# Stick-breaking attention: all projections behind the weighted sums and dealt 3, 4, 6, 7; scores seven tiles ahead; one block of h read back from DRAM

## The chip, the cores and the metric

One Trainium2 chip, one core. The metric is the device time of one execution in microseconds (us). The kernel before took 1917.51 us, the median of 3 runs.

## What is computed

One layer of a decoder trunk on 2048 tokens of width 1024: h is the RMS-normed and modulated x, p = h @ w_in feeds two groups of 8 heads of 64, an RWKV-7 recurrence and a stick-breaking attention, each gated; both go through w_out. The change sits in the attention and in the projections that run beside it.

```python
def stick_breaking_group(p, sb_g):
    q, k, v, g = jnp.split(p, 4, axis=-1)
    ...
    def block(args):
        z = jnp.einsum('bhqd,bhkd->bhqk', q_blk, k).astype(jnp.float32) * scale
        mask = k_pos[None, :] < q_pos[:, None]
        log_1m = jnp.where(mask, jax.nn.log_sigmoid(-z), 0.0)
        after = lax.cumsum(log_1m, axis=3, reverse=True) - log_1m
        attn = jnp.where(mask, jnp.exp(jax.nn.log_sigmoid(z) + after), 0.0)
        return jnp.einsum('bhqk,bhkd->bhqd', attn.astype(v.dtype), v)
    ...
    o = rmsnorm(o, sb_g.reshape(H, N)).reshape(B, S, SB_WIDTH)
    return o * jax.nn.silu(g)
```

## The kernel before

The program has three stretches. The **setup** (0 to 139 us) reads x and the modulation weights, makes h in four blocks of 512 tokens (`make_h`, L262), each as a float16 high part `hh` and low part `hl` of 1 MB that stay in SBUF for the whole program (`hth`, `htl`), and projects q, k, v of the first two blocks. The **attention** (139 to 1045 us) follows, then a second scheduling context with the **RWKV** group and the output projection (1045 to 1918 us).

The attention runs in 16 steps n = 4j + b: j is a pair of heads, b a block of 512 queries. Step n has 8(b+1) items (8, 16, 24, 32). An item is one score tile and one weighted-sum tile, on every engine:

- `scores` (L481): TensorE makes z with two matmuls (L492, L493) into one of 3 PSUM buffers; ScalarE takes two sigmoids, u (L496) and s (L497); GpSimd copies a carry (L507); VectorE runs the cumulative product over u (L505 on the diagonal, L508 elsewhere); GpSimd multiplies it onto s (L509). s has NS = 8 buffers, u has NU = 5.
- `turn` (L514): TensorE transposes up to four 128x128 pieces of s into one of 2 PSUM buffers `tr` (L521); ScalarE copies them out as the high part ah (L525), VectorE makes the low part al (L526).
- `weigh` (L529): TensorE adds ah and al times v into av (L539, L540). It comes LAG = 3 items after its turn.

`attend` (L573) emits per item the scores of the item LEAD = 5 places later, a turn and a weigh. It reaches into the next step except from a step with b = 0, whose successor starts with five score tiles of its own. When a step's second head is done, VectorE writes L550 and TensorE transposes the result (L558, `otp`).

Beside it `fill` (L633) emits the projections: k, q, v of a later step, the gates "g" (attention) and "r" (RWKV) of four blocks each, and, in the last step, four shifted projections z (`pss`). A projection (`inproj`, L351) is 8 pieces of 3 matmuls 128x512. Per head pair 20 of them are dealt to the four steps as 4, 4, 6, 6; the step n = 2 has 3. `_merge` interleaves both lists by planned work, and the scheduler, which runs a timeline model of its own, then sets each engine's order. `pace` (L349) is a scheduling bound: no piece is placed ahead of the weighted sum emitted last before it. It is set from step 12 on (L541) and only for `inproj`, not for `inproj_tok`, which makes v:

```python
        ins = PE.matmul(av[:, r], vs, al[:, r], start=False, stop=last, skip_group_check=True)
        if n >= 12:
            pace[0] = ins.ins
```

All loads and stores named here are issued by SyncE (SP), in order, on one queue.

Of the kernel before, what the change touches and what calls it, by code (L numbers as in the profile page):

```python
# [63 lines left out]
class _Slots:  # L64
# [6 lines left out]
    def tile(self, shape, dtype, name, tag=None, bufs=None):  # L71
        tag = tag or name
        n = self.bufs if bufs is None else bufs
        ring = self.rings.setdefault(tag, [[], 0])
        size = math.prod(shape[1:]) * (2 if dtype in (F16, BF16) else 4)
        if len(ring[0]) < n:
            ring[0].append(self.used[0])
            self.used[0] += -(-size // 32) * 32
            assert self.used[0] <= 4 * self.words
        o = ring[0][ring[1] % n]  # L80
        ring[1] += 1
        key = (o, str(dtype), tuple(shape))
        if key not in self.made:
            self.made[key] = self.nc.alloc_sbuf_tensor_at(f"kept_{name}{o}", shape, dtype, offset=self.base + o)
        t = self.made[key]
        return t[tuple(slice(None) for _ in shape)]


def trunk(nc, a, out):
# [93 lines left out]
    hth, htl = [], []  # L183
    xblk = {}

# [76 lines left out]
    def make_h(b):  # L262
# [14 lines left out]
        hh = hp.tile([P, KB, TB], F16, tag="hth", name="hh")  # L277
        hl = hp.tile([P, KB, TB], F16, tag="htl", name="hl")
# [9 lines left out]
        hth.append(hh)  # L288
        htl.append(hl)
# [61 lines left out]
    def inproj(w, b, name):  # L351
        wh, wl = w[0], w[1]
        ps = mm_ps(name)
        for k in range(KB):
            with tc.issue_after(pace[0]) if pace[0] is not None else nullcontext():
                PE.matmul(ps, wh[:, k], hth[b][:, k], start=k == 0, stop=False)  # L356
            PE.matmul(ps, wh[:, k], htl[b][:, k], start=False, stop=False)  # L357
            PE.matmul(ps, wl[:, k], hth[b][:, k], start=False, stop=k == KB - 1)  # L358
            yield 0.65
        return ps  # L360

    def inproj_tok(w, b, name):
        wh, wl = w[0], w[1]
        ps = mm_ps(name)
        for i in range(4):
            t = slice(i * P, (i + 1) * P)
            for k in range(KB):
                PE.matmul(ps[:, t], hth[b][:, k, t], wh[:, k], start=k == 0, stop=False)
                PE.matmul(ps[:, t], hth[b][:, k, t], wl[:, k], start=False, stop=False)
                PE.matmul(ps[:, t], htl[b][:, k, t], wh[:, k], start=False, stop=k == KB - 1)  # L370
                if k % 4 == 3:
                    yield 0.65
        return ps
# [93 lines left out]
    NS, NU, LEAD, LAG = 8, 5, 5, 3  # L467
# [13 lines left out]
    def scores(n, i, sb):  # L481
# [13 lines left out]
        s = sb.tile([P, TB], F32, tag="s", bufs=NS, name="s")  # L495
# [33 lines left out]
    def weigh(sb, n, i, ah, al, r):  # L529
# [11 lines left out]
        if n >= 12:  # L541
            pace[0] = ins.ins
# [30 lines left out]
    def attend(n, sb):  # L573
# [59 lines left out]
    def fill(n, sb):  # L633
# [3 lines left out]
        if n < 2:  # L637
            m = n + 2
        else:
            m = n + 1 if 2 < n < NST - 1 else None  # L640
        new = b == 3 and not end
        if b == 0 and j > 0:
            yield from w_split("g", j)
# [3 lines left out]
        if b == 3:  # L647
            yield from w_split("z" if end else "k", 0 if end else j + 1)
            w_load("rk" if end else "q", 0 if end else j + 1)
        gates = [("g", 0)], [("g", 1)], [("g", 2), ("g", 3), ("r", 0)], [("r", 1), ("r", 2), ("r", 3)]  # L650
        gates = [proj_g(kind, j, gb, sb) for kind, gb in gates[b]]
        if m is not None:
            yield from proj_k(m)
            if new:
                yield from gates.pop(0)
                yield from w_split("q", j + 1)
                w_load("v", j + 1)
            yield from proj_q(m)
            if new:
                yield from gates.pop(0)  # L660
                yield from w_split("v", j + 1)
                w_load("g", j + 1)
            yield from proj_v(m)
        if j > 0:
            yield from combine(j - 1, b, sb)
        if n == NST - 1:
            for i in range(4):
                yield from proj_z(i, sb)
                if gates:
                    yield from gates.pop(0)  # L670
                if i < 3:
                    yield from w_split(("rk", "rr", "rv")[i], 0)
                if i < 2:
                    w_load(("rr", "rv")[i], 0)
        for g in gates:
            yield from g
        if b == 1:
            w_load("r", j)

    def fill_work(n):  # L680
        b = n % NB
        if n == NST - 1:
            return 5.2 * 7 + 1.5
        return 5.2 * ((4, 4, 6, 6)[b] - 3 * (n == 2)) + 0.9 * (n > 3) + (0.2, 0, 0.2, 0.6)[b]
# [509 lines left out]

    _merge((stage_pw(0), 22), (combines(), 6))
# [4 lines left out]
    def load_wout(k2):  # L1200
        wh = hp.tile([P, 2, D], F32R, tag="hth", name="woh")
        wl = hp.tile([P, 2, D], F32R, tag="htl", name="wol")
# [119 lines left out]
```

## Time and profile before

| | |
|---|---|
| median of 3 runs | 1917.51 us (1916.39 to 1922.70) |
| the profiled execution | 1919.86 us, of which 1918.1 us is the span of instructions |
| attention, 139.0 to 1045.1 us | 906.1 us |
| busy, whole span | PE 89%, DVE 72%, ACT 45%, POOL 40% |
| mean granted TensorE clock | 0.971 of 2.4 GHz |

A stretch's bound is read by putting beside its length what each engine needs for its work there. A busy TensorE is not one at its peak: matmuls overlap in the records, and an isolated one is longer than one in a row. So TensorE's work is counted from its instructions and the distance of the starts of neighbours in a dense run.

### The profile page before, as it was taken

To read this page: it belongs to the slowest core of one execution; us is meant where nothing else is said; L and a number is where in the kernel's file an instruction comes from. 1 tells how busy PE (TensorE), PEld (TensorE's weight loads), DVE (VectorE), ACT (ScalarE), POOL (GpSimd) and SP (SyncE) were. 2 spreads that over 40 slices of the span, in tenths; PEclk is the share of its full clock that TensorE was granted. 3 is DMA by queue.
4 is the path that set the end of the run, shared out by engine and by line. 5 is a ranking of instruction groups with operands and counts; after the bars stand their busy time and mean duration, and the time that the engine had idled before them with its cause. 6 is when DMAs were issued, how large, how long until landed. Compare 5 with 4: busy or idle time off the path is not lost. (4 is left out here: it accounts for less than half of the span.)

```text
span 1918.1 us, 38809 instructions
## 1 busy us (share of the span) xinstructions
PE 1699.1 (89%) x14816; PEld 1164.2 (61%) x14816; DVE 1380.4 (72%) x2871; ACT 859.7 (45%) x1706; POOL 774.4 (40%) x1114
## 2 busy tenths in 40 slices
PE   1879978999899998999997888898899998989998
PEld 1546655666565665667654455665565655667886
DVE  8967697678785778768766557878777777765543
ACT  0556576456564666546644333333332333422221
POOL 3615465356553556445444123233233322223322
PEclk9989999999999999999989989999999999999999
DMA  8341201222122221132111523322332333335442
GB/s 296 112 144 45 70 25 45 64 75 64 42 56 75 61 67 41 51 79 69 54 45 39 154 49 86 69 62 77 77 80 77 86 78 104 80 92 169 149 138 88
DMA packets 210408, 159.93 MB, mean 83 GB/s; under 512 B 113247, under 2 KB 171820, under 8 KB 210222
## 3 DMA queue, kind: packets, MB, share of 16 engines
q1 hardware_dynamic: 209220, 155.31, 28.8%
q8 instruction: 117, 1.92, 0.4%
q10 hardware_dynamic: 1002, 2.13, 0.4%
q14 instruction: 69, 0.57, 0.1%
HBM read 94.48 MB, written 44.04 MB: 72 GB/s over the span
## 5 line engine op out<-in xcount | busy, mean ns | idle before, releaser
L509 POOL TENSOR_TENSOR s<-s,u 128x512 f32<-128x512 f32 (+2 forms) x320 | 306.0, 964 | 219.6 <-ACT s L497 99.7
L526 DVE TENSOR_TENSOR al<-tr,ah 128x512 fp32r<-128x512 f32 (+1 forms) x320 | 187.3, 598 | 98.0 <-ACT ah L525 97.2
L508 DVE TENSOR_TENSOR_SCAN u<-u,dmask 128x512 f32<-128x512 f32 x192 | 239.8, 1267 | 13.7 <-ACT u L496 12.1
L525 ACT ACTIVATE ah<-tr 128x512 fp32r<-128x512 f32 (+1 forms) x320 | 171.9, 553 | 104.8 <-PE tr L521 101.5
L496 ACT ACTIVATE u<-z 128x512 f32<-128x512 f32 (+2 forms) x320 | 173.4, 556 | 73.4 <-PE z L493 48.1
L521 PE MATMUL tr<-kept_ident,s 128*128 128x128 f32 x1088 | 174.2, 280 | 32.8 <-DVE al L526 26.2
L497 ACT ACTIVATE s<-z 128x512 f32<-128x512 f32 (+2 forms) x320 | 166.2, 549 | 54.6 <-PE tr L521 54.6
L521 PEld LDWEIGHTS tr<-kept_ident,s 128*128 128x128 f32 x1088 | 130.9, 143 | 74.5 <-DVE al L526 37.5
L356 PE MATMUL pss<-kept_hh,kept_wh 128*128 128x512 f16 x416 | 160.4, 386 | 8.8 <-PEq L716 8.8
L357 PE MATMUL pss<-kept_hl,kept_wh 128*128 128x512 f16 x416 | 160.3, 385 | 0.0
L358 PE MATMUL pss<-kept_hh,kept_wl 128*128 128x512 f16 x416 | 160.3, 385 | 0.0
L358 PEld LDWEIGHTS <-kept_wl 128*128 128x128 f16 x928 | 93.3, 101 | 105.1 <-issue 14.2
L356 PEld LDWEIGHTS <-kept_wh 128*128 128x128 f16 x928 | 94.5, 102 | 101.5 <-issue 29.8
L357 PEld LDWEIGHTS <-kept_wh 128*128 128x128 f16 x928 | 93.3, 100 | 92.8 <-issue 23.1
L492 PE MATMUL z<-kt,qt 128*128 128x512 f32 (+2 forms) x320 | 132.2, 418 | 10.4 <-ACT s L497 4.4
L539 PE MATMUL av<-ah,vt 128*128 128x512 f32 (+1 forms) x320 | 136.6, 427 | 4.8 <-DVE o L550 2.3
L540 PE MATMUL av<-al,vt 128*128 128x512 f32 (+1 forms) x320 | 136.3, 427 | 0.2 <-DVE al L526 0.2
L493 PE MATMUL z<-kt,qt 128*128 128x512 f32 (+2 forms) x320 | 117.5, 371 | 0.0
L505 DVE TENSOR_TENSOR_SCAN u<-u,dmask 128x128 f32<-128x128 f32 (+3 forms) x128 | 107.2, 866 | 12.2 <-ACT u L496 6.6
L356 PE MATMUL psg<-kept_hh,kept_wh 128*128 128x512 f16 x256 | 100.4, 392 | 8.2 <-DVE klo L420 3.1
L1260 PE MATMUL po<-kept_woh,kept_yh 128*128 128x512 f32 x256 | 103.3, 404 | 0.0
L1261 PE MATMUL po<-kept_wol,kept_yh 128*128 128x512 f32 x256 | 101.9, 398 | 0.0
(292 smaller groups left out, 4167.0 us busy)
## 6 DMA issues: line engine op xcount, KB each, us to landing
kept_raw<-in_w_in SPq DMA_DIRECT2D x29, 512.0 KB, 3.9
ad<-in_ada_w SPq DMA_DIRECT2D x24, 512.0 KB, 5.4
qt<-qt SPq DMA_DIRECT2D x48, 256.0 KB, 3.4
xt<-in_x SPq DMA_DIRECT2D x16, 512.0 KB, 5.2
y<-sg SPq DMA_DIRECT2D x32, 256.0 KB, 2.0
t<-dt SPq DMA_DIRECT2D x64, 128.0 KB, 3.1
xr<-in_x SPq DMA_DIRECT2D x16, 512.0 KB, 3.6
out<-xr SPq DMA_DIRECT2D x16, 512.0 KB, 2.6
```

The source lines that it names most:

```text
L356: PE.matmul(ps, wh[:, k], hth[b][:, k], start=k == 0, stop=False)
L357: PE.matmul(ps, wh[:, k], htl[b][:, k], start=False, stop=False)
L358: PE.matmul(ps, wl[:, k], hth[b][:, k], start=False, stop=k == KB - 1)
L496: A.activation(out=u[:, 0:nk], in_=z[:, 0:nk], func=AF.Sigmoid, scale=-0.125)
L497: A.activation(out=s[:, 0:nk], in_=z[:, 0:nk], func=AF.Sigmoid, scale=0.125)
L508: V.tensor_tensor_scan(out=ur, data0=ur, data1=mr, initial=u[:, nk:nk + 1], op0=ALU.mult, op1=ALU.bypass)
L509: G.tensor_tensor(out=s[:, 0:nk], in0=s[:, 0:nk], in1=u[:, 1:nk + 1], op=ALU.mult)
L521: PE.transpose(tp[:, q * P:(q + 1) * P], att[gi, q][:, ks * P:(ks + 1) * P], ident)
L525: A.activation(out=ah[:, r], in_=tp[:, r], func=AF.Copy)
L526: V.tensor_tensor(out=al[:, r], in0=tp[:, r], in1=ah[:, r].bitcast(F32), op=ALU.subtract)
L539: PE.matmul(av[:, r], vs, ah[:, r], start=first, stop=False, skip_group_check=True)
L540: ins = PE.matmul(av[:, r], vs, al[:, r], start=False, stop=last, skip_group_check=True)
```

## The change

1. Every weighted sum sets `pace`, so all projections of the attention, v among them, are held behind the weighted sums.
2. The 20 projections of a head pair are dealt 3, 4, 6, 7; the last step gets 8 instead of 7. Their order over the blocks changes with it.
3. LEAD goes from 5 to 7, NS from 8 to 12, NU from 5 to 9. The lookahead crosses every step; it waits, in the order of emission, until the q it needs has been projected.
4. Room for it: block 3's buffers of h become eight s buffers. Setup stores each block of h to DRAM (`hd`, 2 MB a block in two DMAs) and puts block 3 where block 0 was. In each head pair block 0 is read back over block 3 in step b = 2, and block 3 over block 0 (over block 1 in the last) in step b = 3; the RWKV part begins by reading block 1 back (`h_load`, two DMAs of 1 MB each).

```diff
+    hth = [hp.tile([P, KB, TB], F16, tag="hth", name="hh") for _ in range(4)]
+    htl = [hp.tile([P, KB, TB], F16, tag="htl", name="hl") for _ in range(4)]
+    hd = [nc.dram_tensor(f"hd{b}", [2, P, KB, TB], F16, kind="Internal").ap() for b in range(NB)]
...
+    def h_load(b, i):
+        for o in [o for o in hat if hat[o] == i]:
+            del hat[o]
+        hat[b] = i
+        for m in range(2):
+            DMA.dma_start(out=hblk(b)[m], in_=hd[b][m])
...
-        hth.append(hh)
-        htl.append(hl)
+        for m in range(2):
+            DMA.dma_start(out=hd[b][m], in_=(hh, hl)[m])
...
-    NS, NU, LEAD, LAG = 8, 5, 5, 3
+    NS, NU, LEAD, LAG = 12, 9, 7, 3
+    skept = [t[:, i] for t in (hp.at("hth", 3, [P, 4, TB], F32, "s"), hp.at("htl", 3, [P, 4, TB], F32, "s"))
+             for i in range(4)]
...
-        if n >= 12:
-            pace[0] = ins.ins
+        pace[0] = ins.ins
...
-        ahead = LEAD if n % NB else 0
-        if n % NB == 1 or n == 0:
+        if n == 0:
             for p in range(p0, p0 + LEAD):
                 yield scores(*seq[p], sb)
         for p in range(p0, p1):
-            if p + LEAD < min(p1 + ahead, len(seq)):
+            if p + LEAD < len(seq):
+                while seq[p + LEAD][0] not in qst:
+                    yield 0.02
                 yield scores(*seq[p + LEAD], sb)
...
+        if b == 0:
+            yield from kqv(n + 1 if j > 0 else 2)
+        if b == 1:
+            yield from kqv(n + 1 if j > 0 else 3)
+            yield from g("g", 2 if j > 0 else 3)
...
+            yield from g("r", 3)
+            h_load(0, hat[3])
+            yield from g("r", 2)
...
+            yield from g("g", 0)
+            yield from g("r", 0)
+            h_load(3, hat[0])
+            yield from g("r", 1)
...
-            return 5.2 * 7 + 1.5
-        return 5.2 * ((4, 4, 6, 6)[b] - 3 * (n == 2)) + 0.9 * (n > 3) + (0.2, 0, 0.2, 0.6)[b]
+            return 5.2 * 8 + 1.7
+        return 5.2 * ((3, 4, 6, 7)[b] - 3 * (n == 2)) + 0.9 * (j > 0) + (0.2, 0, 0.2, 0.6)[b]
...
+    h_load(1, 3)
     _merge((stage_pw(0), 22), (combines(), 6))
```

How the instructions stand after it. Rows of the change carry its own line numbers; z, tr, av, psg are the PSUM tiles of scores, transposes, weighted sums and gate projections.

TensorE near the end of step n = 2 (24 items). Before:

```order
L539 MATMUL av<-ah,vt 128x512
L521 MATMUL tr<-kept_ident_61,s 128x128 x4
L540 MATMUL av<-al,vt 128x512
L492 MATMUL z<-kt,qt 128x512
L493 MATMUL z<-kt,qt 128x512
L319 MATMUL wtp<-kept_wl_238,kept_ones_66 128x128
```

With the change:

```order
L570 MATMUL av<-ah,vt 128x512
L552 MATMUL tr<-kept_ident_61,kept_s_238 128x128 x4
L571 MATMUL av<-al,vt 128x512
L380 LDWEIGHTS kept_wh_806
L380 MATMUL psg<-kept_hh_110,kept_wh_806 128x512
L381 LDWEIGHTS kept_wh_806
L381 MATMUL psg<-kept_hl_114,kept_wh_806 128x512
L382 LDWEIGHTS kept_wl_807
L382 MATMUL psg<-kept_hh_110,kept_wl_807 128x512
```

Before, the last 20 weighted sums before this step ends stand on TensorE without a projection between them. Now a piece or two of a gate projection stands behind nearly every weighted sum up to the step's end.

SP at the end of setup: the modulation row `gr` goes to DRAM. Before:

```order
L203 DMA ad<-in_ada_w 128x1024 x4
L422 DMA kt<-kt 64x512
L423 DMA kt<-klo 64x512
L424 DMA kt<-klo 64x512
L604 DMA gdram<-gr 1x1024
L408 DMA qt<-qt 64x1024
```

With the change:

```order
L224 DMA ad<-in_ada_w 128x1024 x5
L312 DMA hd<-kept_hh_111 128x4096
L312 DMA hd<-kept_hl_115 128x4096
L448 DMA kt<-kt 64x512
L449 DMA kt<-klo 64x512
L450 DMA kt<-klo 64x512
L312 DMA hd<-kept_hh_109 128x4096
L312 DMA hd<-kept_hl_113 128x4096
L635 DMA gdram<-gr 1x1024
```

The stores of blocks 2 and 3 of h now stand ahead of the row's store; those of block 3 stand right ahead of it.

SP in step n = 6 (b = 2) of the change, around the reading back of block 0:

```order
L469 DMA y_3<-sg 128x512
L205 DMA kept_hl_113<-hd 128x4096
L205 DMA kept_hh_109<-hd 128x4096
L469 DMA y_3<-sg 128x512
L469 DMA y_2<-sg 128x512
L481 DMA ol<-odram 128x4x128
```

The two loads stand between the stores of the two gate projections of block 3 and behind nothing else that is new; the stores of gates and a load of `combine` stand behind them.

## Rows read from the trace of the kernel before

**Rows 1.** The page: span, and busy time of each engine.

```profile
span 1918.1 us, 38809 instructions
...
PE 1699.1 (89%) x14816; PEld 1164.2 (61%) x14816; DVE 1380.4 (72%) x2871; ACT 859.7 (45%) x1706; POOL 774.4 (40%) x1114
```

**Rows 2.** Timeline of DVE: the L550 that ends step n = 7.

```profile
591.15 0.68 DVE L550 TENSOR_TENSOR o<-av,olo 64x512 f32<-64x512 f32 x1
```

**Rows 3.** Stretches: length, busy PE, PEld, DVE, ACT, POOL, clock, DMA share, GB/s.

```profile
139.00:218.30 79.30, 72.77 (x515) 51.79 (x514) 55.13 (x78) 48.93 (x110) 42.91 (x95) 0.96 0.24 52
218.30:274.70 56.40, 45.70 (x236) 31.41 (x236) 46.30 (x66) 38.36 (x82) 33.81 (x62) 0.97 0.09 29
274.70:364.70 90.00, 81.41 (x488) 54.37 (x489) 69.15 (x104) 51.94 (x106) 46.67 (x79) 0.96 0.17 45
364.70:393.10 28.40, 26.15 (x210) 18.09 (x209) 14.44 (x23) 10.41 (x24) 10.11 (x19) 1.00 0.42 110
393.10:441.60 48.50, 48.47 (x332) 33.40 (x331) 36.53 (x53) 30.94 (x67) 27.18 (x51) 1.00 0.24 61
441.60:502.90 61.30, 56.40 (x374) 39.12 (x372) 49.48 (x69) 40.74 (x86) 34.52 (x63) 0.99 0.19 53
502.90:591.80 88.90, 82.03 (x491) 56.27 (x492) 70.06 (x106) 51.89 (x106) 47.43 (x80) 0.95 0.18 51
591.80:822.30 230.50, 213.45 (x1404) 146.05 (x1403) 171.51 (x251) 134.18 (x282) 118.29 (x209) 0.98 0.22 60
822.30:896.00 73.70, 71.74 (x528) 50.71 (x526) 51.15 (x76) 41.39 (x90) 37.35 (x70) 1.00 0.29 77
896.00:959.20 63.20, 59.23 (x388) 41.15 (x388) 50.46 (x72) 41.59 (x86) 33.19 (x61) 1.00 0.22 61
959.20:1045.10 85.90, 79.27 (x387) 48.20 (x387) 61.60 (x109) 45.70 (x88) 38.71 (x54) 0.94 0.13 41
```

**Rows 4.** Timeline of PE, dense runs: start, length, line.

```profile
154.94 0.93 PE L521 MATMUL tr<-kept_ident,s 128*128 128x128 f32 x7
...
157.69 0.38 PE L357 MATMUL psg<-kept_hl,kept_wh 128*128 128x512 f16 x1
157.90 0.38 PE L358 MATMUL psg<-kept_hh,kept_wl 128*128 128x512 f16 x1
...
164.50 0.39 PE L493 MATMUL z<-kt,qt 128*128 128x512 f32 x1
164.73 0.40 PE L492 MATMUL z<-kt,qt 128*128 128x512 f32 x1
```

**Rows 5.** PE's waits in the attention: total us, times, longest.

```profile
PE tr L521 <- DVE al L526: 26.2, 26, 2.2
```

**Rows 6.** ACT's waits in the attention for buffers that GpSimd frees.

```profile
ACT u L496 <- POOL u L507: 9.8, 6, 2.9
...
ACT u L496 <- POOL s L509: 2.3, 3, 1.9
```

**Rows 7.** Timeline of PE in step 7, the longest wait for a tr buffer.

```profile
553.88 0.47 PE L539 MATMUL av<-ah,vt 128*128 128x512 f32 x1
556.52 1.01 PE L521 MATMUL tr<-kept_ident,s 128*128 128x128 f32 x4 [2.17 <-DVE al L526]
```

**Rows 8.** End of setup: timeline of SP, then of ACT.

```profile
138.68 0.26 SPq L604 DMA_DIRECT2D gdram<-gr  x1
...
140.27 0.28 ACT L496 ACTIVATE u<-z 128x128 f32<-128x128 f32 x1 [3.01 <-DMA gdram<-gr]
```

**Rows 9.** A stretch of setup (columns of rows 3); DMA issues, KB, us to landing.

```profile
20.00:30.00 10.00, 0.15 (x1) 0.00 (x0) 9.84 (x23) 0.00 (x0) 8.92 (x7) 1.00 1.05 390
...
y<-sg SPq DMA_DIRECT2D x32, 256.0 KB, 2.0
```

**Rows 10.** Start of the RWKV part: timeline of SP, then of PE.

```profile
1055.74 0.58 SPq L455 DMA_DIRECT2D kept_both<-odram  x1
...
1060.63 0.55 PE L462 MATMUL tr<-kept_ident,kept_both 128*128 128x128 f32 x3
```

More of the change, by code (lines that the diff above doesn't have):

```diff
@@ L81, in tile, with at, _view @@
         ring[1] += 1
+        return self._view(o, shape, dtype, name)
+    def at(self, tag, i, shape, dtype, name):
+        return self._view(self.rings[tag][0][i], shape, dtype, name)
+    def _view(self, o, shape, dtype, name):
         key = (o, str(dtype), tuple(shape))
@@ L352, in inproj @@
         wh, wl = w[0], w[1]
+        hh, hl = hblk(b)
         ps = mm_ps(name)
@@ L636, in fill, with g, kqv @@
         end = j == NB - 1
[L637 to L643, printed above, removed]
+        def g(kind, gb):
+            return proj_g(kind, j, gb, sb)
+        def kqv(m):
+            yield from proj_k(m)
+            yield from proj_q(m)
+            yield from proj_v(m)
+        if b == 0:
+            if j > 0:
+                yield from w_split("g", j)
+            w_load("r", j)
+            yield from kqv(n + 1 if j > 0 else 2)
+        if b == 1:
+            yield from kqv(n + 1 if j > 0 else 3)
+            yield from g("g", 2 if j > 0 else 3)
         if b == 2:
@@ L646, in fill @@
             w_load("z" if end else "k", 0 if end else j + 1)
[L647 to L663, printed above, removed]
+            if j > 0:
+                yield from kqv(n + 1)
@@ L664, in fill @@
+            yield from g("g", 3 if j > 0 else 2)
+            yield from g("r", 3)
+            h_load(0, hat[3])
+            yield from g("r", 2)
         if j > 0:
             yield from combine(j - 1, b, sb)
-        if n == NST - 1:
[L667 to L682, printed above, removed]
-            return 5.2 * 7 + 1.5
-        return 5.2 * ((4, 4, 6, 6)[b] - 3 * (n == 2)) + 0.9 * (n > 3) + (0.2, 0, 0.2, 0.6)[b]
+        if b == 3 and not end:
+            yield from w_split("k", j + 1)
+            w_load("q", j + 1)
+            yield from g("g", 1)
+            yield from proj_k(n + 1)
+            yield from w_split("q", j + 1)
+            w_load("v", j + 1)
+            yield from proj_q(n + 1)
+            yield from w_split("v", j + 1)
+            w_load("g", j + 1)
+            yield from proj_v(n + 1)
+            yield from g("g", 0)
+            yield from g("r", 0)
+            h_load(3, hat[0])
+            yield from g("r", 1)
@@ new lines, in fill @@
+        if b == 3 and end:
+            yield from w_split("z", 0)
+            w_load("rk", 0)
+            yield from proj_z(0, sb)
+            yield from proj_z(1, sb)
+            yield from g("g", 1)
+            yield from g("r", 1)
+            h_load(3, hat[1])
+            yield from w_split("rk", 0)
+            w_load("rr", 0)
+            yield from g("g", 0)
+            yield from g("r", 0)
+            yield from w_split("rr", 0)
+            w_load("rv", 0)
+            yield from proj_z(2, sb)
+            yield from w_split("rv", 0)
+            yield from proj_z(3, sb)
```

34 lines of the change are left out of this document (22 added, 12 removed).

## The prediction

> **What bounds the kernel now.** I read the page first. TensorE is busy 89% of the span, VectorE 72% [rows 1]. Such a share over the whole program says little, so next I cut the attention into its steps. The cut is where VectorE writes the second head's result (L550), as for step 7 at 591.15 + 0.68 us [rows 2], and each stretch shows what the engines did [rows 3]. The reader should see there that the attention is not one regime. The stretch of a b = 1 step (393.1 to 441.6) is full on TensorE, 48.47 of 48.5 us. The b = 2 and b = 3 stretches (441.6 to 591.8) are not, and VectorE is at about 80% in them. In the stretch of n = 2, with three projections for 24 items, VectorE is busy 46.3 of 56.4 us.
>
> Busy is not work, so I count TensorE's work. In dense runs the starts of projection matmuls lie 0.21 to 0.22 us apart, those of score matmuls 0.23, and seven transposes take 0.93, which is 0.28 for a lone one and 0.108 for each that follows [rows 4]. A projection is thus 24 x 0.216 = 5.2 us. Counting every matmul between the finishing transposes of two steps, before and with the change (the order of instructions gives the counts, these spacings the times):
>
> - b = 0: 25.5 before, 21.7 with the change
> - b = 1: 45.3, then 41.7
> - b = 2: 50.6, then 60.0
> - b = 3: 78.4, then 76.4
>
> The whole attention stays at 776 us of TensorE work, so the change can only win idle time: 906.1 - 776 = 130 us at most. I do the same for VectorE, each instruction at its mean duration, scaled to the busy time that the rows show; for these four kinds of stretch it goes from 14, 37, 50, 70 us to 23, 29, 51, 70.
>
> The waits say what makes the idle time. TensorE's largest one is a transpose that waits for VectorE to empty one of the two tr buffers: 26.2 us in 26 waits [rows 5]. ScalarE waits 9.8 + 2.3 us for GpSimd to free u and s buffers [rows 6]. The change adds u and s buffers, not tr buffers.
>
> **Part 1: pacing, dealing and lookahead together.** They shift work between the stretches, so I price them through stretch length over TensorE work, and how that goes with VectorE's load (its busy time over the same work), from steps 4 to 7 [rows 3]: b = 1 has load 0.81 and ratio 48.5 / 45.3 = 1.07; b = 3 has 0.89 and 1.13; b = 2 has 0.98 and 1.21. Step n = 2 has VectorE as its bound, and a length of 1.22 times VectorE's busy time. The idle time grows as the two loads come near each other. With the change:
>
> - b = 0: VectorE's 23 us are the larger, 23 x 1.22 = 28 (before 28.4).
> - b = 1: load 0.69, ratio 1.05, 43.8 (48.5).
> - b = 2: load 0.85, ratio 1.10, 66 (61.3). It gets 9.4 us of work and pays 4.7.
> - b = 3: load 0.91, ratio 1.14, 87 (88.9).
>
> The sum is 224.8 against 227.1: -2 for steps 4 to 7. Steps 8 to 11 are the same program and took 230.5: -6. Steps 12 and 13: 28 + 43.8 against 73.7: -2. Step 14 has 54.2 of work at load 0.94, ratio 1.17: 63.4 against 63.2, nothing. Step 15 goes from 68.7 to 73.4 of work, since it gets the eighth projection; it has no later step to reach into, so I keep its excess: 8 us of drain over 1.12 times the work, 90 against 85.9: +4. Steps 0 and 1 go from 72.8 to 62.6 of work; load 0.91, ratio 1.14, 71.4 against 79.3: -8. Step 2 gets 46.6 of work instead of 34.2, with VectorE still at 48: 1.22 x 48 = 58.5 against 56.4: +2. Step 3: 76.4 of work, load 0.86, ratio 1.11: 85 against 90: -5. Sum of part 1: **-17**.
>
> **Part 2: what the lookahead and its buffers do to the ratios themselves.** The rows cannot show this, since before has no deeper lookahead. At one end it does nothing: the tr buffers stay two and the projections still stand in runs of six to ten pieces in a b = 3 step. At the other end it takes all 26.2 us of the tr waits, because scans done earlier let VectorE reach the tr copy sooner. A wait costs more than itself: after one of 2.17 us the four transposes took 1.01 us [rows 7] instead of 0.28 + 3 x 0.108 = 0.60, and the granted clock of these stretches is 0.95 [rows 3]; so that end is about 35. The nearest row is ScalarE's 12.1 us of buffer waits [rows 6], which the new buffers do address. I take **-10**, range 0 to -35. A loss here is not excluded, as more scans ready early can stand ahead of a tr copy; up to +5.
>
> **Part 3: storing and reading back h.** Eight loads of 2.1 MB happen in the attention. The first use of the block read back stands about 31 us of TensorE work behind the load in both places. Such a load takes 5.4 us at the 390 GB/s of setup's densest stretch and 16 us at the rate of a lone 256 KB store in 2.0 us [rows 9]. Both fit: 0. SP waits for the last matmul that reads the old block before it issues a load. Behind it stand the same projection's gate store, another gate store and a load for `combine`; the first has to wait for that projection anyway, and nobody on TensorE waits for the others for ten us. With the stores these are 24 DMAs, about half a us of SP each; SP's queue is far from full.
>
> Two places are not covered. **At the end of setup** the first sigmoid waits for the store of `gr`: issued at 138.68, sigmoid at 140.27 [rows 8]. Block 3's stores, 2.1 MB, now go out right ahead of it. The end of setup moves little else: the other stores fall into time with free DMA. If the row's store goes around them the cost is the issue, 0.5 us; if it waits for them, 5.4 us at setup's rate [rows 9], 16 at the slowest. I take **+5.5**, as both kinds of DMA are from one queue. The Trainium skill, in "DMA: Bandwidth & Descriptors", section "Queues, rings and completion order", says that each DMA engine takes a ring's descriptors in order and that a completion lands only after all earlier writes of that engine. By that rule the row waits, which is what I take; by its table in "Bandwidth", 6.15 us per MB, the term would be about an estimated 12. No run here shows it yet.
>
> **At the start of the RWKV part** block 1 (2.1 MB) is read ahead of `combine`'s load. That load went out at 1055.74 and its transposes ran at 1060.63 [rows 10]. Now 2.1 MB, 5.4 us at setup's rate, lie ahead of it, while its transposes stand twelve groups of three matmuls into the part instead of five, seven times 0.65 us later. I take **+2**, between 0 and 8. The rest of that part has the same order of matmuls.
>
> **The sum.** -17 - 10 + 5.5 + 2 = -19.5. The profiled execution took 1919.86 us, 1.7 of them outside its span, and stands 2.3 above the median of 1917.51. So 1919.9 - 19.5 gives about **1900 us**; from the median it would be 1898.
>
> **The rivals.**
>
> - *The ratios improve much more* (chance 0.20). Projections spread behind every weighted sum keep VectorE fed, and a third of the 130 us of idle time goes: -43 + 8, 1885 us. For it: the end of step 2, where 20 weighted sums stood bare. Against it: steps 12 to 14 were paced before, and their 136.9 us for 122.9 of work are no better a ratio (1.11) than steps 4 to 6 with 138.2 for 121.4 (1.14) by much.
> - *No change* (0.17). The deal only moves work between stretches: j = 0 gives 11, step 15 takes 4, setup and RWKV take 8. About 1919 us. For it: tr stays at two buffers.
> - *Slower* (0.15). The b = 2 step keeps its ratio of 1.21 although it gets one and three quarters more projections, because it is VectorE's order of scans and tr copies that paces it, not its load. Then 60.0 becomes 72.6 in steps 6 and 10, and 54.2 becomes 65.6 in 14: +15 on part 1; with nothing from part 2 and the full 16 + 8 of part 3 that is +22, 1942; with my part 3 it is +5.5. It decides from a b = 2 ratio of about 1.16 on (9.5 us over 174 of work), with part 2 at nothing.
>
> **How the numbers follow.** The first case has 0.48. A measurement of this kernel can tell about 0.3%, 5.75 us. Faster by more: 0.43 of the first case, 0.20 of the second, 0.02 of the third, so 0.65. Slower: 0.13 and 0.04, so 0.17. Within: 0.18. The range goes from the second case with a little more, 1876, to 1928, which leaves out the far half of the slow case and a tail of the fast one.
>
> **What would show each step.** The first sigmoid near 146 us instead of 140.3 (part 3). The b = 2 stretches about 66 us long, b = 0 and 1 together about 72 (before 76.9), the first two steps about 71 us. TensorE's tr waits under 26 us, ScalarE's waits on L507 nearly gone. The RWKV part within a few us of 873. I am wrong if a wait of TensorE on a read-back block of h shows, if b = 2 takes 70 us or more, or if the b = 3 stretches drop under 82 us.

## The result and the profile after

The changed kernel takes **1930.23 us**, median of 11 runs, against 1917.35 for the kernel before, run in turn with it: ratio 1.0078, 95% interval 1.0058 to 1.0098. By the ratio it is slower by 0.8%, some 15 us; the two medians lie 12.9 us apart, and the 11 runs of the changed kernel spread from 1927.38 to 1940.56. The forecast was 1900, faster; the time lies above its range, 1876 to 1928, as well.

The page of the changed kernel, span and TensorE, VectorE, ScalarE, GpSimd:

```profile
span 1929.2 us, 38851 instructions
...
PE 1703.5 (88%) x14816; PEld 1168.9 (61%) x14816; DVE 1377.3 (71%) x2871; ACT 862.4 (45%) x1706; POOL 773.4 (40%) x1114
```

Beside [rows 1] the work is the same; only the span grew, by 11.1 us. The stretches, cut as in [rows 3] (length, busy PE, PEld, DVE, ACT, POOL, clock, DMA share, GB/s): j = 0, then j = 1, then the last step.

```profile
139.00:171.60 32.60, 26.95 (x201) 21.49 (x202) 24.53 (x35) 22.49 (x57) 22.33 (x62) 0.84 0.17 46
171.60:211.30 39.70, 39.20 (x288) 28.91 (x286) 31.81 (x46) 27.19 (x60) 23.73 (x40) 1.00 0.34 71
211.30:266.60 55.30, 50.24 (x267) 32.84 (x265) 48.75 (x68) 40.23 (x82) 36.08 (x65) 1.00 0.19 67
266.60:359.50 92.90, 82.86 (x487) 54.36 (x488) 65.78 (x103) 49.78 (x103) 40.96 (x69) 0.96 0.24 74
359.50:393.10 33.60, 30.43 (x216) 21.98 (x214) 23.05 (x32) 18.94 (x44) 19.30 (x40) 0.90 0.30 81
393.10:435.20 42.10, 40.34 (x290) 28.61 (x290) 28.96 (x43) 24.18 (x52) 19.09 (x34) 1.00 0.24 62
435.20:501.70 66.50, 64.18 (x404) 44.91 (x404) 50.15 (x66) 40.87 (x84) 34.89 (x63) 0.97 0.29 89
501.70:595.60 93.90, 82.76 (x494) 54.20 (x495) 69.40 (x111) 51.38 (x105) 44.80 (x76) 0.98 0.24 72
...
971.40:1057.00 85.60, 80.62 (x409) 49.22 (x409) 62.12 (x113) 46.08 (x89) 34.74 (x51) 0.98 0.21 69
...
1057.00:1929.20 872.20, 781.02 (x8958) 538.63 (x8958) 584.70 (x1652) 270.98 (x501) 251.36 (x229) 0.97 0.35 97
```

The attention goes from 906.1 to 918.0 us; the RWKV part stays, 872.2 against 873.0. The first three steps are 8.1 us shorter than before. Then j = 1 takes 236.1 us against 227.1: b = 0 is 5.2 longer, b = 1 6.4 shorter, b = 2 5.2 and b = 3 5.0 longer.

I call *idle* the length of a stretch less its matmuls at the spacings of [rows 4] (0.216 us for 512 columns of a projection, 0.23 for 512 columns of a score or a weighted sum, fewer columns in proportion, 0.108 for a transpose); a low clock is in it. In j = 1 it goes from 3.5, 1.5, 8.2, 14.3 us (b = 0 to 3) to 8.1, 3.6, 6.1, 18.7, and over the whole attention from 131 to 143, which is the loss. So it is TensorE waiting or running slowly, not more work. Its waits, 139 to 1057 us (total, times, longest), and then one row of ScalarE's:

```profile
PE tr L552 <- DVE al L557: 28.6, 37, 1.9
PE z L522 <- DMA qt<-qt: 8.9, 6, 2.1
...
PE psq L382 <- DVE kept_wl L358: 2.3, 2, 1.2
...
PE wtp L342 <- ACT kept_wl L340: 1.6, 2, 0.9
...
ACT u L527 <- POOL kept_s L540: 0.9, 1, 0.9
```

Before, the two kinds that grew most stood at:

```profile
PE z L492 <- DMA qt<-qt: 1.9, 1, 1.9
...
PE psv L369 <- DVE kept_wl L335: 1.3, 2, 1.1
```

The tr waits are about where they were (26.2, [rows 5]), although ScalarE's waits for u and s buffers [rows 6] have gone to 0.9 us. What grew are the waits of scores for the copies of q, and those for split weights. A b = 0 step shows the first kind (PE, then SP):

```profile
606.75 0.22 PE L396 MATMUL psv<-kept_wh,kept_hl 128*128 128x128 f16 x1
606.78 0.30 PE L571 MATMUL av<-al,vt 128*128 128x128 f32 x1
609.03 0.30 PE L522 MATMUL z<-kt,qt 128*128 128x128 f32 x1 [1.94 <-DMA qt<-qt]
...
605.63 0.46 SPq L436 DMA_DIRECT2D qt<-qt  x1
```

The last copy of q is issued at 605.63. At 607.1 the v projection and the last weighted sum are done, and TensorE has nothing until the copy lands.

A second cost stands behind the first. In the b = 0 step of j = 1, TensorE waits 1.66 us for q and starts again at 372.59; two us later it runs at the lower of its two clock levels, 1.2 GHz, for 6.8 us:

```profile
372.59 0.30 PE L522 MATMUL z<-kt,qt 128*128 128x128 f32 x1 [1.66 <-DMA qt<-qt]
...
374.50:381.30 6.80, 6.33 (x22) 4.67 (x20) 6.62 (x9) 6.46 (x13) 5.31 (x14) 0.50 0.36 116
```

The granted clock of the b = 0 steps of j = 1 to 3 is thus 0.90, 0.95 and 0.95, where before it was 1.00, 0.94 and 1.00. The idle time of a b = 0 step holds both, the wait and the slow stretch.

The end of setup, SP and then ScalarE, beside [rows 8]:

```profile
134.93 0.33 SPq L312 DMA_DIRECT2D hd<-kept_hh  x1
135.69 0.33 SPq L312 DMA_DIRECT2D hd<-kept_hl  x1
136.29 0.89 SPq L635 DMA_DIRECT2D gdram<-gr  x1
...
141.68 0.28 ACT L527 ACTIVATE u<-z 128x128 f32<-128x128 f32 x1 [6.78 <-DMA gdram<-gr]
```

The row's store reaches the sigmoid 5.4 us after its issue, before 1.6. The setup got there 2.4 us earlier, so the first sigmoid is 1.4 us later.

### The profile page after: what moved, and what is told of

It is laid out like the page before. It is cut to its first block, busy times and chain, and to the rows that moved or that the text cites. A ratio compares the mean times of both kernels' runs of the same rounds, so it can differ in the third digit from the quotient of the medians.

```text
span 1929.2 us, 38851 instructions
## 1 busy us (share of the span) xinstructions
PE 1703.5 (88%) x14816; PEld 1168.9 (61%) x14816; DVE 1377.3 (71%) x2871; ACT 862.4 (45%) x1706; POOL 773.4 (40%) x1114
## 5 line engine op out<-in xcount | busy, mean ns | idle before, releaser
L540 POOL TENSOR_TENSOR kept_s<-kept_s,u 128x512 f32<-128x512 f32 (+1 forms) x216 | 205.3, 954 | 146.6 <-ACT kept_s L528 39.0
L522 PE MATMUL z<-kt,qt 128*128 128x512 f32 (+2 forms) x320 | 134.8, 424 | 21.1 <-DMA qt<-qt 8.9
L552 PE MATMUL tr<-kept_ident,kept_s 128*128 128x128 f32 x726 | 118.8, 282 | 20.0 <-DVE al L557 17.8
L540 POOL TENSOR_TENSOR s<-s,u 128x512 f32<-128x512 f32 (+2 forms) x104 | 101.5, 982 | 67.7 <-ACT s L528 24.6
L536 DVE TENSOR_TENSOR_SCAN u<-u,dmask 128x128 f32<-128x128 f32 (+3 forms) x128 | 107.4, 867 | 29.6 <-ACT u L527 20.8
L528 ACT ACTIVATE kept_s<-z 128x512 f32<-128x512 f32 (+1 forms) x216 | 117.3, 553 | 11.5 <-PE tr L552 11.3
L523 PE MATMUL z<-kt,qt 128*128 128x512 f32 (+2 forms) x320 | 120.0, 379 | 0.0
L552 PEld LDWEIGHTS tr<-kept_ident,kept_s 128*128 128x128 f32 x726 | 88.2, 144 | 49.3 <-DVE al L557 25.2
L356 POOL TENSOR_TENSOR kept_raw<-kept_raw,rkw 128x1024 f32<-128x1024 f32 x29 | 55.3, 1908 | 137.2 <-DVE rkw L355 119.1
```

The source lines that it names most:

```text
L522: PE.matmul(z[:, 0:nk], qt[:, h, 0, qs], kt[:, h, 0:nk], start=True, stop=False)
L540: G.tensor_tensor(out=s[:, 0:nk], in0=s[:, 0:nk], in1=u[:, 1:nk + 1], op=ALU.mult)
L552: PE.transpose(tp[:, q * P:(q + 1) * P], att[gi, q][:, ks * P:(ks + 1) * P], ident)
```

## The experiments

A ratio is that to the kernel before in runs in turn with it on one chip, with its 95% interval. The four lengths are those of the steps b = 0 to 3 of j = 1, each from one profiled execution.

| kernel | ratio (interval) | b = 0, 1, 2, 3, us |
|---|---|---|
| before | 1 | 28.4, 48.5, 61.3, 88.9 |
| after | 1.0078 (1.0058 to 1.0098) | 33.6, 42.1, 66.5, 93.9 |
| no_cross | 1.0013 (0.9995 to 1.0031) | 20.7, 52.3, 64.0, 92.4 |
| weights_apart | 0.9975 (0.9953 to 0.9998) | 35.4, 41.9, 66.6, 88.3 |
| apart_no_cross | 0.9947 (0.9929 to 0.9965) | 20.8, 53.0, 64.5, 88.7 |
| deal_only | 1.0118 (1.0090 to 1.0146) | 26.5, 48.7, 67.3, 95.6 |
| deal_pace | 1.0096 (1.0066 to 1.0126) | 27.4, 45.9, 65.4, 96.4 |
| before_3467 | 1.0061 (1.0040 to 1.0083) | 22.3, 53.1, 62.2, 97.8 |
| pace_only | 0.9920 (0.9895 to 0.9944) | 31.9, 44.0, 62.7, 89.9 |
| no_pace | 1.0078 (1.0051 to 1.0105) | 40.3, 41.0, 63.3, 91.4 |
| deal_pace_h | 1.0161 (1.0137 to 1.0185) | 29.4, 46.0, 66.6, 96.1 |
| h_reads | 1.0062 (1.0038 to 1.0085) | 27.2, 48.0, 65.0, 96.8 |
| buffers_only | 1.0079 (1.0052 to 1.0107) | 29.4, 47.4, 67.8, 91.0 |
| before_tight | 0.9933 (0.9910 to 0.9956) | 24.3, 48.5, 61.3, 86.7 |
| tight_pace | 0.9900 (0.9866 to 0.9934) | 32.0, 44.2, 62.8, 90.2 |
| deal_apart | 1.0081 (1.0053 to 1.0108) | 23.2, 52.0, 66.5, 93.1 |
| apart_4466 | 1.0013 (0.9995 to 1.0031) | 32.6, 44.5, 65.5, 86.4 |
| apart_4466_no_cross | 0.9992 (0.9975 to 1.0010) | 34.4, 46.4, 64.2, 85.7 |
| old_deal_look | 0.9989 (0.9967 to 1.0012) | 36.7, 46.8, 63.2, 86.3 |
| old_deal_look_late | 0.9988 (0.9964 to 1.0012) | 36.5, 48.2, 63.8, 88.6 |

### The deal and the pacing

deal_only, on the kernel before (`fill` and `fill_work` are those of the change, without its `h_load`):

```diff
-        return 5.2 * ((4, 4, 6, 6)[b] - 3 * (n == 2)) + 0.9 * (n > 3) + (0.2, 0, 0.2, 0.6)[b]
+        return 5.2 * ((3, 4, 6, 7)[b] - 3 * (n == 2)) + 0.9 * (j > 0) + (0.2, 0, 0.2, 0.6)[b]
```

> Only part 2 of the change, the deal 3, 4, 6, 7 and its order of blocks, on the kernel before; all four blocks of h stay resident, LEAD 5, 8 and 5 buffers, pacing from step 12 on. Theory DEAL (the deal itself costs: with three projections the b = 0 stretch runs out of TensorE work, and in b = 3 the weight splits stand between paced pieces): 1927 to 1932 us, b = 0 stretches of 32 to 34 us and b = 3 of 93 to 95. Theory LOOKAHEAD (the deeper lookahead and its buffers cost): 1905 to 1917, b = 3 at 87 to 90. Theory PACE (holding all projections costs): 1905 to 1917. Theory TRAFFIC (stores and reads of h cost): 1905 to 1917.

1944.28 us, 1.0118, above all four ranges: the deal by itself loses at least as much as the whole change does. Of the four theories DEAL alone allowed a loss. b = 3 is at 95.6 as it said, but b = 0 is at 26.5, not at 32 to 34; so its account of b = 0 is not right for the short lookahead.

deal_pace adds to that:

```diff
-        if n >= 12:
-            pace[0] = ins.ins
+        pace[0] = ins.ins
...
+                with tc.issue_after(pace[0]) if pace[0] is not None else nullcontext():
+                    PE.matmul(ps[:, t], hh[:, k, t], wh[:, k], start=k == 0, stop=False)
```

> Parts 1 and 2 of the change: the deal and the pacing of all projections, v among them; LEAD 5, 8 and 5 buffers, all of h resident. Theory PACE: some 13 us above the run with the deal alone, 1925 to 1932. Theory DEAL: the same as the deal alone, 1927 to 1932. Theories LOOKAHEAD and TRAFFIC: 1905 to 1917.

1941.13 us, 1.0096, again above the ranges. The pacing costs nothing on top; PACE falls. This is most of what the forecast priced in its part 1 at -17 us: it measures +18. The scans that the long lookahead moves into b = 0, and which part 1 priced too, are not in it.

pace_only is that second edit on the kernel before.

> The kernel before with part 1 alone, all projections paced. Theory PACE: 1.003 to 1.010, since held projections can't fill the gaps ahead of them. From the pairs measured with the deal (1.0118 to 1.0096) and with everything (1.0078 both ways): 0.997 to 1.001.

1908.91 us, **0.9920**: pacing alone is worth 15 us, better than either range. In its profile all of the gain in the attention (896.8 us for 906.1) lies in the first three steps, 125.8 us instead of 135.7:

```profile
139.00:174.40 35.40, 31.90 (x232) 23.06 (x231) 24.27 (x35) 22.91 (x57) 19.96 (x56) 0.95 0.17 42
174.40:213.40 39.00, 37.92 (x275) 27.19 (x273) 30.03 (x44) 25.95 (x54) 23.22 (x38) 1.00 0.33 69
213.40:264.80 51.40, 44.88 (x246) 31.25 (x246) 47.22 (x67) 39.39 (x82) 34.57 (x63) 1.00 0.10 32
```

no_pace takes it out of the changed kernel.

```diff
-        pace[0] = ins.ins
+        if n >= 12:
+            pace[0] = ins.ins
...
-                with tc.issue_after(pace[0]) if pace[0] is not None else nullcontext():
```

> The changed kernel without part 1: pacing from step 12 on and for inproj alone, as before; the deal, the lookahead, the crossing and the read-back stay. Theory PACE (holding projections costs): 1915 to 1922. From the pair deal and deal with pacing, where pacing gave 3 us: 1930 to 1936. With a deep lookahead and no hold, projections can run ahead and leave the ends of steps bare: b = 2 over 66.5, b = 3 over 94.

1942.37 us, 1.0078, the ratio of the changed kernel; the time is over all that was expected, but b = 2 and b = 3 did not get longer. n = 2 goes from 55.3 to 60.5 and b = 0 of j = 1 from 33.6 to 40.3, b = 3 from 93.9 to 91.4; its profiled attention is 11.4 us longer (929.4 against 918.0). Ratio and profile do not say the same, so what the pacing is worth in the changed kernel stays open.

before_3467 tells the numbers of the deal from its order:

```diff
-        gates = [("g", 0)], [("g", 1)], [("g", 2), ("g", 3), ("r", 0)], [("r", 1), ("r", 2), ("r", 3)]
+        gates = [], [("g", 1)], [("g", 2), ("g", 3), ("r", 0)], [("r", 1), ("r", 2), ("r", 3), ("g", 0)]
```

In its last step the moved gate comes after its weights' buffer was given to the weights of rv, and multiplies by those; the instructions are the same in number and size.

> The kernel before with g of block 0 moved from b = 0 to the end of b = 3: 3, 4, 6, 7 projections, 8 in the last step, all else as it was. Theory DEAL (the numbers cost: b = 3 is VectorE's and takes the added projection at full price, b = 0 and b = 1 don't get shorter): b = 3 at 93 to 96, b = 0 and b = 1 together 74 to 76, ratio 1.006 to 1.010. If the order of kinds and blocks costs, not the numbers: 0.995 to 1.002.

1936.18 us, 1.0061. The numbers alone cost about half of the deal's loss. Its b = 0, 1 and 3 stretches of j = 1:

```profile
370.00:392.30 22.30, 17.96 (x162) 14.34 (x161) 9.48 (x18) 7.17 (x18) 6.81 (x14) 0.92 0.38 94
392.30:445.40 53.10, 53.10 (x356) 36.02 (x355) 41.06 (x58) 33.83 (x73) 30.36 (x55) 1.00 0.25 68
...
507.60:605.40 97.80, 85.84 (x515) 56.99 (x516) 71.67 (x107) 52.91 (x107) 47.27 (x80) 0.98 0.18 49
```

A projection of 5.2 us left b = 0; b = 0 and 1 together got 1.5 us shorter, and b = 3 got 8.9 longer. The idle time of b = 0 rose from 3.5 to 7.1, that of b = 3 from 14.3 to 18.0. In b = 0 TensorE's waits that the profile names rise from 2.1 to 4.3 us and the granted clock falls from 1.00 to 0.92; in b = 3 the named waits rise from 8.2 to 13.3 us, 2.1 of them for split weights (0.2 before). So work taken from the one place left gaps there, and in the other it brought waits with it.

### The lookahead

buffers_only, from h_reads (below), has 12 and 9 buffers and LEAD 5; no_cross has LEAD 7 as well and is the changed kernel but for:

```diff
+        ahead = LEAD if n % NB else 0
-        if n == 0:
+        if n % NB == 1 or n == 0:
...
-            if p + LEAD < len(seq):
+            if p + LEAD < min(p1 + ahead, len(seq)):
```

> As the run with 9 and 5 buffers, but 12 s and 9 u buffers; LEAD stays 5 and the lookahead doesn't cross a b = 0 step. If the buffers alone give what the lookahead gives (ScalarE no longer waits for GpSimd to free them): 1922 to 1930. If LEAD 7 does it (the run without crossing, 1924 to 1927, has both): within 4 us of the run with 9 and 5 buffers.

> The changed kernel, but the lookahead doesn't reach out of a b = 0 step, as before; LEAD 7, 12 and 9 buffers stay. Theory CROSSING (a part of LOOKAHEAD: scores of the b = 1 step wait in a b = 0 step for q and its copies, and bring VectorE's scans into the shortest stretch): b = 0 back to 26 to 29 us, b = 1 at 42 to 47, in all 1915 to 1922. If the crossing isn't it, 1927 to 1933, with b = 0 and b = 1 together still 75 to 76 us.

1943.29 us, 1.0079, and 1926.57 us, 1.0013. The buffers do nothing by themselves; seven tiles instead of five are worth 0.66%, some 13 us. Part 2 of the forecast, -10, was right in size as long as the lookahead doesn't reach out of a b = 0 step. TensorE's waits for tr buffers and for copies of q, in the attention of buffers_only and then of no_cross, where none for q is left:

```profile
PE tr L552 <- DVE al L557: 31.9, 32, 2.7
PE z L522 <- DMA qt<-qt: 9.8, 3, 3.4
...
PE tr L552 <- DVE al L557: 23.4, 38, 2.5
```

That the lookahead does reach out costs the same 0.65% again, between no_cross and the changed kernel:

```profile
358.10:378.90 20.80, 18.41 (x172) 14.01 (x171) 10.21 (x21) 8.57 (x21) 6.55 (x14) 1.00 0.47 124
378.90:431.20 52.30, 50.66 (x342) 35.55 (x340) 43.99 (x59) 35.81 (x78) 34.88 (x67) 1.00 0.21 54
```

b = 0 and 1 take 73.1 us here and 75.7 with the crossing; the expectation had their sum, but not 20.8 and 52.3 by themselves. VectorE has 10.2 us of work in this b = 0 and 23.05 in the changed kernel's, but the idle time is 3.5 against 8.1: the scores that cross stand behind k, q and q's copies, with one projection left beside them. Of the 13.6 us that the attention of this profile is shorter, 12.3 lie in j = 1 to 3; but this execution took 1916.27 us, 10 us less than the median of its kernel.

Two things keep this from being the price of the crossing alone. Idle time of b = 0 is not peculiar to it: deal_pace, h_reads and buffers_only do not cross and have 7.9, 7.6 and 8.4 us there, buffers_only with longer waits for q. And without the crossing the end of setup comes out in another order, the row's store between the two stores of block 3. The sigmoid then follows 3.1 us after the row's issue, not 5.4, which is 2.3 of the 12 us (SP, then ScalarE, of no_cross):

```profile
133.44 0.33 SPq L312 DMA_DIRECT2D hd<-kept_hh  x1
134.43 0.24 SPq L636 DMA_DIRECT2D gdram<-gr  x1
135.03 0.71 SPq L312 DMA_DIRECT2D hd<-kept_hl  x1
...
137.56 0.28 ACT L527 ACTIVATE u<-z 128x128 f32<-128x128 f32 x1 [4.15 <-DMA hd<-kept_hh]
```

### The place of the weight splits

weights_apart, on the changed kernel:

```diff
             yield from w_split("q", j + 1)
             w_load("v", j + 1)
+            yield from g("g", 0)
             yield from proj_q(n + 1)
             yield from w_split("v", j + 1)
             w_load("g", j + 1)
+            yield from g("r", 0)
             yield from proj_v(n + 1)
-            yield from g("g", 0)
-            yield from g("r", 0)
```

> The changed kernel with one edit: in a b = 3 step a gate projection stands between the splitting of the weights of q and v and the projection that uses them (g of block 0 ahead of q, r of block 0 ahead of v), as gates did in the kernel before. The profile of the changed kernel has its idle TensorE time of these steps in their first 55 us, at the transposes and the matmuls that wait for split weights, and none in the last 35 us, where the gates stand in a row. Theory WEIGHTS (the order of the deal puts each weight split right ahead of its projection): b = 3 from 93 to 94.4 down to 88 to 90, 1915 to 1920 in all. If the b = 3 idle time is VectorE's and not the weights': 93 to 95 still, 1927 to 1933.

One thing in it is not so: in the kernel before, a gate stands ahead of each of these splits, and the split right ahead of its projection, as in the change.

1922.29 us, **0.9975**: 1.0% under the changed kernel. j = 1, b = 0 and 3:

```profile
351.80:387.20 35.40, 30.09 (x216) 20.94 (x214) 23.04 (x33) 18.93 (x44) 19.40 (x40) 0.95 0.31 82
...
495.70:584.00 88.30, 81.04 (x494) 54.29 (x495) 67.28 (x110) 51.67 (x105) 43.21 (x75) 0.98 0.26 76
```

All three b = 3 steps before the last lose 5.6 to 6.5 us, and no projection of theirs waits for kept_wl any more. b = 0 keeps its idle time, 9.8 us.

apart_no_cross has both edits.

> The run with the weights apart, and without the crossing of a b = 0 step. If the two losses are separate (weights: ratio 0.9975 against 1.0078, so 20 us; crossing: 1.0013 against 1.0078, so 12 us), the gains add: about 0.991 of the kernel before, b = 0 and b = 1 together 73, b = 3 at 86 to 88. If the scores that cross only move the same idle time about, it stays at 0.995 to 0.998.

1911.33 us, **0.9947**: of 1.7% that the two would give one by one 1.3% come, between the two cases of the expectation. It beats the kernel before and the changed one.

deal_apart is the same edit on deal_only. before_tight changes the kernel before; it does not move a split away from its projection or towards it, but takes the gate out from ahead of the split and puts it behind v:

```diff
             if new:
-                yield from gates.pop(0)
                 yield from w_split("q", j + 1)
...
             if new:
-                yield from gates.pop(0)
                 yield from w_split("v", j + 1)
```

> The run with the deal alone, and its weights apart; all of h resident, LEAD 5, old pacing. Theory WEIGHTS: the deal's 1.012 falls by about the same 1% to 1.000 to 1.004, b = 3 from 93 to 95.6 down to 88 to 90. If the deal 3, 4, 6, 7 costs in itself (the shortest stretches left with the least work): it stays over 1.007.

> The kernel before with one edit: in b = 3 the splits of q's and v's weights stand right ahead of their projections, and the three gates of the step come after v, as the deal of the change has them. Theory WEIGHTS: b = 3 from 89 to 91 up to 94 to 96, ratio 1.005 to 1.010. If the order alone is harmless and only the pacing or the read-back makes it cost: within 0.3% of the kernel before.

1937.56 us, 1.0081, and 1909.09 us, **0.9933**. In deal_apart the splits stand apart and the loss stays, over 1.007 as its second case says, with b = 3 at 93.1. In before_tight they stand right ahead of their projections, as before, with no gate ahead of them, and the kernel before gets 0.7% faster, its b = 3 at 86.7. With both, theory WEIGHTS falls. In before_tight TensorE does wait twice in b = 3 of j = 1 at the small matmul of a split (`wtp`, 2.6 us), and for a tr buffer only once:

```profile
PE wtp L319 <- ACT kept_wl L317: 2.6, 2, 2.1
PE otp L558 <- DVE o L550: 1.4, 1, 1.4
PE tr L521 <- DVE al L526: 0.9, 1, 0.9
```

against 4.2 us of tr waits in this stretch before. The place of the splits by itself is not what costs. What else differs between these kernels is the order of instructions that comes out; that this is the cause is argued, not shown.

tight_pace adds the pacing.

> The kernel before with all projections paced, and with the weight splits right ahead of their projections, gates last. Theory HELD WEIGHTS (a split costs where its projection is held in its place): b = 3 from 88 to 91 (paced alone) up to 94 to 96, ratio 1.000 to 1.006. If the gains of the two edits add (0.992 and 0.9933): 0.983 to 0.988, b = 3 at 85 to 88.

1905.56 us, **0.9900**, the lowest ratio of all, though its interval overlaps with those of pace_only and before_tight. HELD WEIGHTS falls too: b = 3 stays at 90.2, where pacing alone has 89.9. The two gains do not add fully (0.985).

### The traffic of h

deal_pace_h is deal_pace with stores, read-back and the slot of h as eight s buffers:

```diff
+        for m in range(2):
+            DMA.dma_start(out=hd[b][m], in_=(hh, hl)[m])
...
-        s = sb.tile([P, TB], F32, tag="s", bufs=NS, name="s")
+        s = skept[made[0] % NS] if made[0] % NS < 8 else sb.tile([P, TB], F32, tag="s", bufs=NS - 8, name="s")
```

With eight of these and LEAD 5, tile i + 8 is written before the last transposition of tile i was issued, so that this one reads the wrong tile; the amount of work is the same.

> Parts 1, 2 and 4: as the run with deal and pacing, but three slots of h with the stores and the read-back, and eight s buffers in the fourth slot; LEAD 5, 5 u buffers. Theory TRAFFIC: 10 us or more above the run with deal and pacing, with TensorE waits on a block of h or longer waits for q. The forecast's part 3 (5.5 at the end of setup, 2 at the start of the RWKV part): 7 us above it. If h is free: within 3 us of it. Theory LOOKAHEAD: 1905 to 1920, since the lookahead is still the short one.

1953.16 us, 1.0161. Since the order between scores and transpositions is another one there, it doesn't price the traffic. h_reads does, with a ninth s buffer beside the eight:

> Deal, pacing and read-back of h with LEAD 5, no crossing of b = 0, 9 s and 5 u buffers (eight s buffers in the slot of h, one beside). Against the run with deal and pacing alone (1941) it prices the traffic of h. Theory TRAFFIC: 1949 to 1955. If h is free: 1938 to 1944. Forecast's part 3: 1948.

1939.14 us, 1.0062 (1.0038 to 1.0085), against 1.0096 (1.0066 to 1.0126) without any traffic: no cost of h shows, and TRAFFIC falls. In the changed kernel a load of 1 MB lands 4.7 to 9.0 us after its issue, and no engine waits for one:

```profile
DMA to landing us min/median/max: 4.7/7.0/9.0
```

### Other deals with the long lookahead

apart_4466 and apart_4466_no_cross, from weights_apart and apart_no_cross:

```diff
         if b == 0:
...
+            if j > 0:
+                yield from g("g", 1)
...
         if b == 3 and not end:
...
-            yield from g("g", 1)
+            yield from g("g", 0 if j > 0 else 1)
```

> The run with the weights apart, crossing kept, but from the second head pair on the gate g of block 1 stands in b = 0 instead of b = 3: 4, 4, 6, 6 projections as before (7 in the last step). Theory: the b = 0 stretch of 35.4 us with 21.7 us of work is long because the scores that cross wait for k, q and q's copies, and one projection (v) is all that TensorE has meanwhile. Then the added 5.2 us of work fit into it: b = 0 stays at 34 to 36 and b = 3 falls by 4 to 6 us, 12 to 15 us in all, 0.990. If the stretch is paced by VectorE and the order, b = 0 grows by 4 to 5 us and nothing is won.

> As the one before, without the crossing. If the crossing is the cause of the b = 0 idle time, b = 0 (20.7 us without it) takes the gate at full price, 26 us, b = 3 gives it back, and the time is that of the run with the weights apart and no crossing within 0.2%.

1925.17 us, 1.0013, and 1922.37 us, 0.9992; both slower than without the edit. The first half of the expectation holds: with one more projection b = 0 gets shorter, 35.4 to 32.6, its idle time falls from 9.8 to 3.0. But b = 3 gives back 2, not 5, and b = 1 takes 2.6. In its profile j = 1 to 3 are 3 us shorter and j = 0 is 6.6 longer, because that execution's setup ended 6.6 us later with the same instructions. Without the crossing the expectation fails: b = 0 takes 34.4 us, not 26, and the time is 0.5% over that of apart_no_cross. Why the medians are higher isn't settled.

old_deal_look and old_deal_look_late have LEAD 7, 12 and 9 buffers, no crossing and read-back with the numbers and kinds of the kernel before (`fill` anew, blocks 0, 1, 2 at the start of a head pair, block 3 over 1 and back).

```diff
+        if b == 1:
+            yield from g("g", 1 if j > 0 else 3)
+            if j > 0:
+                h_load(3, hat[1])
...
+            yield from g("r", 3)
+            h_load(*((1, hat[3]) if j > 0 else (0, hat[3])))
```

> Lookahead 7 with 12 and 9 buffers, no crossing, read-back of h and pacing as in the change, but 4, 4, 6, 6 projections in the order of kinds of the kernel before (k, gate, q, gate, v, gate in b = 3), with blocks chosen so that three slots do (two reads in each head pair). If the deal itself costs 0.8% beside the weights: 0.987 to 0.991. If lookahead and deal have to go together: 0.994 to 1.000.

> As the one before, with pacing from step 12 on alone, as in the kernel before. If pacing is worth nothing: within 0.3% of it. If a long lookahead needs the pacing, so that projections don't run ahead: 0.5 to 1% slower, as ends of steps with b = 2 and b = 3 stand bare.

1919.15 us, 0.9989, and 1920.76 us, 0.9988. With the old numbers the long lookahead is no gain: old_deal_look is 0.7% slower than pace_only. With the new numbers it gained 0.8% (deal_pace to no_cross). That lookahead and deal depend on each other is one reading. It is not shown, for old_deal_look also has the traffic of h and another order of blocks, and in the profiles its whole loss in the attention lies in the first three steps (140.3 us against 125.8; from there on 771.1 against 771.0).

## Why the prediction was wrong

**Part 1 failed**, and in it the terms of b = 3 and of b = 0. The loads were forecast well: VectorE has 23.05, 28.96, 50.15 and 69.40 us of work in the four stretches of j = 1, where the text had 23, 29, 51, 70. The lengths were not: 33.6, 42.1, 66.5, 93.9 where the text had 28, 43.8, 66, 87. Over the attention the terms of b = 3 ahead of the last step are 22 us too low and those of b = 0 17 us; b = 1, step 2 and the last step together give back some 13. With part 2's -10 that is the way from -27 to the +11.9 us that the attention took.

**The step at fault** is "The idle time grows as the two loads come near each other", used as a price. It took one ratio per load from three stretches in one order of instructions. The order is what the change changes. b = 3 of j = 1 has 75.2 to 76.1 us of matmuls in four kernels with the new deal, and its idle time is 20.3 (deal_pace), 21.1 (h_reads), 18.7 (after), 13.1 (weights_apart); with the old deal (74.3 to 75.8 us of matmuls) it is 14.3 (before), 15.6 (pace_only), 10.9 (before_tight). Much the same work of TensorE, 67 to 71 us of VectorE's, and up to twice the idle time: the load does not give the price. That it hangs on which piece stands where when VectorE is late is my reading, not shown. Which pair of instructions decides it, the runs do not settle: TensorE's named waits in this stretch sum to 8.2 us before and 11.0 after, which is 2.8 of the 4.4 us by which its idle time grew.

deal_pace, which has the new deal and the pacing but the short lookahead, tells the two terms apart. Its b = 0 and b = 3 of j = 1:

```profile
364.10:391.50 27.40, 22.45 (x185) 16.73 (x184) 16.59 (x25) 13.00 (x30) 11.13 (x22) 0.94 0.38 97
...
502.80:599.20 96.40, 85.19 (x498) 53.91 (x499) 71.30 (x110) 53.10 (x108) 48.65 (x78) 0.98 0.17 47
```

b = 3 is 9.4 us over the forecast without any long lookahead, and so are step 3 (95.1 for 85) and the last (96.3 for 90); these terms fail by the deal. That b = 0 is 27.4 for 28 there is luck: the 28 were priced from 23 us of VectorE's work, and VectorE has 16.59.

**b = 0** failed in the changed kernel, where those 23 us are: 28 forecast, 33.6 to 34.0 measured, 5.6 to 6.0 us three times. I priced the moved scans and not that the next step's scores need a q of the same step, nor that TensorE runs at 1.2 GHz after such a wait (6.8 us in j = 1). The rule "b = 0 excepted" in the code before was worth its line. no_cross puts it at 0.65%, the 2.3 us at the end of setup among it.

**Part 2** was right in size: -10 taken, about -13 measured for LEAD 7 without the crossing and with this deal. The size is in part luck. The -10 rested on 12.1 us of ScalarE's waits for u and s buffers; with the buffers alone these go from 20.5 us (h_reads) to 1.7 (buffers_only), and nothing is gained. The tr waits did fall with LEAD 7, from 31.9 to 23.4 us, but so did the waits for q, from 9.8 to nothing, which the text did not have; and in the changed kernel the tr waits are 28.6, over the 26.2 of before.

**Part 3.** No cost of h shows in the attention, as said. At the end of setup the row's store waits for the 2.1 MB ahead of it, as taken: 3.8 us more (5.4 against 1.6 us to the sigmoid) for the 5.5 forecast. The Trainium skill, "DMA: Bandwidth & Descriptors", "Queues, rings and completion order", has the rule that a completion lands only after an engine's earlier writes; the trace agrees, and so does no_cross, where one of the two stores is ahead of the row and it takes 3.1 us. By that page's table for loads in "Bandwidth" the two stores would take an estimated 12 us; they and the row were through 6.75 us after the first one's issue (134.93 to 141.68). The RWKV part lost nothing: +2 forecast, 872.2 against 873.0.

**The rivals.** "Slower" was on the list for b = 2 staying at a ratio of 1.21. b = 2 came out at 66.5 for 60.0 of work, 1.11, as in the main case. The slow outcome came from the neighbours, b = 0 and b = 3, which no rival held. Of the signs of being wrong that the text named, a wait on a block read back and a b = 2 of 70 us, neither came; b = 3 was named only for the case that it fell under 82. Of the signs of being right, b = 0 and 1 together at about 72 us (75.7) and tr waits under 26 us (28.6) did not come.

## What to carry to other kernels

Ratios of length to work, read from one schedule, don't price a change of the schedule itself: the same b = 3 step held between 11 and 21 us of idle time here. What could have been read beforehand is dependence: whether work that is brought forward needs something that is made in the same stretch, and whether what is dealt away from a short stretch was the cover of a wait. And a bundle of four edits is worth taking apart: pacing alone gives 0.8%, while the bundle loses 0.8%. The taking apart has a limit of its own here: an edit can make the scheduler set another order far from it, down to one store at the end of setup, so a difference of two runs need not be the price of the edit alone.

## What the runs showed of the hardware

A small store waits for large ones ahead of it on the same queue, by how many there are. From the issue of the 4 KB row to the sigmoid it is 1.6 us in the kernels that do not store h, 3.1 with one 1 MB store right ahead (no_cross) and 5.4 with two (after).

The end of setup, with the same instructions in the same order up to there, came 6.6 us apart in two profiled executions: VectorE's `gr` at 133.31 us (weights_apart) and at 139.89 (apart_4466). At the issue of five loads of modulation weights 5.0 of these are there already:

```profile
115.43 2.32 SPq L224 DMA_DIRECT2D ad<-in_ada_w  x5
...
120.47 2.42 SPq L224 DMA_DIRECT2D ad<-in_ada_w  x5
```

A difference of a few us between two single profiles should not be read into the edit until the stretches show it in every head pair.
